# A block with RWKV-7 heads on one core: doublings of the triangular inverse for two chunks at a time, and three generators for a chunk's preparation instead of two

## The chip, the cores and the metric

The kernel runs on one core of a Trainium2 chip. The metric is the device time of one execution in microseconds (us), as the median over runs.

## What is computed

Two layers of a trunk over 1280 tokens of 1024 features: 256 tokens of context, then 1024 latent ones. Each layer normalises, multiplies by one combined input projection, gives its columns to three groups of heads (gated linear attention, windowed softmax attention, RWKV-7 in both directions), multiplies what they return by one output projection, adds it, and ends with a SwiGLU network. The part that the change touches is the RWKV-7 recurrence, for 4 heads of 64 features and for both directions:

```python
def step(S, inp):
    rt, wt, kt, vt, kkt, at = inp
    sa = jnp.einsum('bhvk,bhk->bhv', S, kkt)
    S = (S * wt[:, :, None, :] - sa[..., None] * (kkt * at)[:, :, None, :]
         + vt[..., None] * kt[:, :, None, :])
    return S, jnp.einsum('bhvk,bhk->bhv', S, rt)
```

The kernel computes it in chunks of 64 tokens. Within a chunk the updates depend on one another through a strictly triangular 64 x 64 matrix N of each head and direction, and the kernel forms the inverse of (I - N). Everything is float32.

## The kernel before, in words

**The stage.** `mixers` runs, in each layer, the RWKV heads beside the rest of the input projection. The projection has 22 column tiles; nine of them (RWKV's own) come before, and 13 are left for this stage. A column tile is 24 MATMULs for each of three groups of tokens (256, 512 and 512 of them); in the second layer some columns leave the group of 256 out. The last of the 13 (`HOLD = 1`) begins only when the last step of the scan is through. In the text these are the dense products; their tile is `ps_in`.

**The planner.** `Weave` (L669 ff.) writes down the order in which TensorE (PE) takes all this; PE then follows that order strictly. The work is in generators. Each one traces some instructions and then yields either the nanoseconds until its next part has its operands, or a condition on other stages (`after`, `known`). The planner keeps a clock of its own, `TE.t`, which every matmul advances by a fixed estimate (a float32 one with up to 32 rows: 1.06 ns a column; other float32 ones: 1.67 ns a column, at least 130 or 215 ns; dense ones: columns / 2.4 ns; a transpose 108 ns). It takes the part that is ready first and, of those that are ready, the one with the lowest rank; dense products have rank 9 and are always ready. One rule stands above that: where less than `SHARE` = 1000 ns of dense products began within the last 3400 ns of its clock, a dense one goes next. `LEAD` (22000 and 20000 ns by layer) is the time for which dense products run alone at the start. The order on the other engines is left to the framework's scheduler.

**A chunk.** There are NC = 20 steps. In each, both directions do one chunk, and a tile holds four units u (direction, pair of heads).

- `load` (L1105): two DMAs bring `AK`, 256 KB each, from DRAM tensor `d_ab`; `Dt` is copied.
- `prep_a` (rank 2): loads one chunk ahead; waits for the scan of three steps before ("s", i - 3); `gram` makes `LQ` from `AK` (8 matmuls and a masked multiplication on VectorE); `X` starts as the identity, is filled by a select (`copy_predicated`) from `ld`, four ScalarE copies of blocks of `LQ`; then two calls of `level`.
- `level` (L1091): 16 products of 32 x 32 into `ps_y`, a ScalarE copy to `y`, 16 products into `ps_w`, a select into `X` and a transpose into `XT` on VectorE. Each doubles the size of the inverted diagonal blocks. A float32 matmul is two records in the trace, so one such group is "x32".
- `prep_b` (rank 1): after "a" of this chunk and the scan of two steps before; loads v (`VU`, `Vbd`, six DMAs); makes `Ke` on GpSimd; a `level`; the second `gram` (`MP`); a `level`; copies to `XF`; the last doubling (`ps_y6`, `ps_w6`, 8 products each); transposes of `Ke` to `KT`.
- `scan` (rank 0): after "b" of this chunk and the step before: `ps_r` (MP times v, AK times the state `SBD`), copies to `Rbd`, U from `X` (L1218), `VU` copied, `ps_s` from `KT`, the new `SBD` (L1227), and the output rows (L1230 ff.).
- `finish_all` (rank 3): norms of finished token tiles.

`X` and `XT` have two buffers each, `LQ` and `VU` three, `AK` and `y` four. All small PSUM tiles of these generators share a ring of three banks.

```python
def level(lv, LQ, X, XT):
    py = new([P, 4, 32], "ps_y")
    ...
    S.copy(y, py)
    yield 1000
    ...
    V.transpose(f2(XT), f2(X))
    yield 1200
```

Of the kernel before, what the change touches and what calls it, by code (L numbers as in the profile page):

```python
# [57 lines left out]
# column tiles of the input projection, in the order in which they are computed  # L58
# [5 lines left out]
# columns of the per-layer parameter tile  # L64
# [81 lines left out]
def block_kernel(ctx: ExitStack, tc: tile.TileContext, a):  # L146
# [3 lines left out]
    class Tensor:  # L150
        """the tensor engine with an estimate of its time, in ns"""
# [48 lines left out]
    # decay over a chunk, by direction and pair of heads  # L200
# [74 lines left out]
    class Norm:  # L275
        """RMS norm over the features, which lie on the partitions and along k of x"""
# [5 lines left out]
        def add(self, o, g0, n):  # L282
            # apart: not of the ring, whose slots go by the order of the program
# [38 lines left out]
        def modulated(self, l, w_, g0, n, h):  # L322
            """h[:, k, 0 / 1, :] = leading and trailing part of modulate(rmsnorm(x))"""
# [31 lines left out]
    def product(ps, n, wh, k0=0, total=None):  # L355
        """ps[:, :n] = sum over pairs of a weight tile (hi, lo) and activations (hi, lo) in float32 accuracy"""
# [7 lines left out]
    def rsqrt(pool, v, name):  # L364
        """1 / sqrt(v) in place of v, a small tile: bit guess and Newton steps"""
# [26 lines left out]
    # (column of a padded tile, token, tokens)  # L392
    PIECES = [(1, 0, 256), (258, 256, 512), (770, 768, 512)]

    def in_rwkv(l, h, wpool, pool, bpool, cpool, pp, beside, first):
        """the columns of RWKV and what is elementwise in it; the results go to DRAM"""
# [17 lines left out]
        # in the last layer the tokens of the context give keys and values only  # L414
# [3 lines left out]
        def conv(*names):  # L418
            """projection and centred shift of columns; tokens at 1:257 and 258:1282"""
# [29 lines left out]
        def scan_inputs(j, o, t0, n, d):  # L449
            """a, r, kappa and beta of a pair of heads and a direction"""  # L450
# [17 lines left out]
            # exp of the decays up to a token, with a one before the first (forward) or after the last (backward)  # L468
# [73 lines left out]
    def tokens_of(aux, tmp, y, t0, n, dst):  # L542
        """the n columns of y, token-major"""
# [7 lines left out]
    def in_rest(l, h, cols, wpool, pool, own, ypool, pp, spawn):  # L551
        """the other columns, step by step"""
# [6 lines left out]
        def drain(nm, g0, n, ps):  # L559
            # not of the ring for the first columns, whose slots go by the order of the program  # L560
# [61 lines left out]
    def in_gla(l, t0, pool, own, pp, dw):  # L622
        """what is elementwise in the linear attention, for 256 tokens"""
# [38 lines left out]
    def known(at, keys):  # L662
        """for a generator in a Weave: waits for all of the keys (stage, number from 0 on)"""
# [5 lines left out]
    class Weave:  # L669
        """Traces generators in the order in which the tensor engine takes their parts. A generator yields the  # L670
        time until its next part has its operands, or a function that returns the time from which on it has
        them (None: not known yet). Of what is ready, the first in the list goes first."""
# [9 lines left out]
        def run(self, manual=True, stay=()):  # L682
            """until all jobs have ended but those of the ranks that may stay"""
            with tc.manual_schedule(engines={mybir.EngineType.PE}) if manual else nullcontext():
                while any(j[0] not in stay for j in self.jobs):
# [11 lines left out]
                    if self.share:  # L697
                        # the dense matmuls are spread so that the engine's clock stays up
# [15 lines left out]
    def column(mh, t):  # L714
        """the columns of a token tile in the tile of its group"""
# [3 lines left out]
    def mixers(ctx_, l, t_first, ins, h, wpool, dpool):  # L719
        """RWKV beside the rest of the input projection"""  # L720
# [25 lines left out]
    def gla_states(d, t, kt, vt, St, gD, ps_of, into, n=2):  # L746
        """the states (head and key, value) behind the first n chunks of a tile, St the one before them"""
# [12 lines left out]
    def gla_backward(pool, keep_, ps_of, spawn):  # L760
        """the states behind every chunk from the right; returns those after the second and the first of a tile"""
# [26 lines left out]
    def gla_mixer(l, t_first, mh, back, pool, late, pp, spawn):  # L788
# [20 lines left out]
        def forward():  # L809
# [5 lines left out]
            for t in range(NT):  # L815
# [82 lines left out]
        # leading and trailing parts of the values side by side  # L898
# [30 lines left out]
    def swa_mixer(l, t_first, mh, loaded, pools, pp, spawn):  # L929
        # in the order in which what is in them ends  # L930
# [9 lines left out]
        def soft():  # L940
            yield 1000
            for i, (b, kv, j) in enumerate(items):
# [9 lines left out]
                # (place, tokens, key, starts a bank)  # L952
# [16 lines left out]
                if kv == j == 0:  # L969
                    # maximum (negative), sum, sink and 1 / sum of the heads  # L970
# [39 lines left out]
        def values():  # L1010
            o_ = None
            for i, (b, kv, j) in enumerate(items):
# [39 lines left out]
    def rwkv_mixer(l, t_first, pool, fpool, pp, spawn):  # L1052
        """units u = (direction, head pair); heads of a pair lie on the two halves of the partitions"""
# [5 lines left out]
        lev = pool.tile([P, 5, 128], U8, name="lev")  # L1059
        for i in range(5):  # L1060
            lf = pool.tile([P, 2, 64], F32, name="lf")
            o = CO["lev"][0] + i * 256
            SY.dma_start(lf, a["cst"][:, o:o + 256].rearrange("p (d n) -> p d n", d=2)[:, :, 0:64])
            V.tensor_copy(lev[:, i, :], lf.rearrange("p d n -> p (d n)"))
# [6 lines left out]
        XF = [pool.tile([P, 4, 64], F32, name=f"XF{i}") for i in range(2)]  # L1071
# [4 lines left out]
        # times from which on the results of the stages of the steps are there  # L1076
# [12 lines left out]
        blocks = [(u, slice(r, r + 32), slice(r % 64, r % 64 + 32)) for u in range(4) for r in (0, 32, 64, 96)]  # L1089
# [528 lines left out]
```

## Time and profile before

| | |
|---|---|
| median of 3 runs | 3871.54 us (3871.51 to 3885.14) |
| span of the profiled execution | 3864.4 us |
| PE busy | 3708.4 us, 96% |
| VectorE (DVE), ScalarE (ACT), GpSimd (POOL) busy | 49%, 38%, 21% |
| stage of the change, layer 0 / layer 1 | about 319 to 765 us / 2327 to 2770 us |

The profile is of one execution, and its time is given as its span, from the first instruction to the last; the runs have a median 7.1 us above it. "PEld" is the loading of weights, which overlaps the products; "granted clock" is the share of TensorE's full speed that it was given in a stretch, 1.00 being full and 0.50 the lower level. A row of a timeline merges neighbouring instructions of one form. A duration of a merged row runs to the end of its last matmul, which overlaps the start of the next row, so the pace is read from one start to the next.

### The profile page before, as it was taken

To read this page: it belongs to the slowest core of one execution; us is meant where nothing else is said; L and a number is where in the kernel's file an instruction comes from. 1 tells how busy PE (TensorE), PEld (TensorE's weight loads), DVE (VectorE), ACT (ScalarE), POOL (GpSimd) and SP (SyncE) were. 2 spreads that over 40 slices of the span, in tenths; PEclk is the share of its full clock that TensorE was granted. 3 is DMA by queue.
4 is the path that set the end of the run, shared out by engine and by line. 5 is a ranking of instruction groups with operands and counts; after the bars stand their busy time and mean duration, and the time that the engine had idled before them with its cause. 6 is when DMAs were issued, how large, how long until landed. Compare 5 with 4: busy or idle time off the path is not lost. (4 is left out here: it accounts for less than half of the span.)

```text
span 3864.4 us, 75751 instructions
## 1 busy us (share of the span) xinstructions
PE 3708.4 (96%) x31194; PEld 2894.2 (75%) x31194; DVE 1888.0 (49%) x3773; ACT 1457.8 (38%) x3054; POOL 821.6 (21%) x1169
## 2 busy tenths in 40 slices
PE   7999899999999999999999998899999999999998
PEld 4547677767788888888887766677777778888887
DVE  4663545566554333333334783455575643433334
ACT  4333543357334323333333443543375231111113
POOL 3111222211323223323332131222112310000002
PEclk9999999989999999999999999999899999999999
DMA  5454443331311122222211244343322211111111
GB/s 206 148 176 128 119 127 106 85 107 34 117 62 55 61 68 69 69 63 67 70 61 60 80 156 122 107 133 98 89 78 85 83 33 50 40 53 44 55 44 60
DMA packets 264826, 334.96 MB, mean 87 GB/s; under 512 B 48417, under 2 KB 197025, under 8 KB 262433
## 3 DMA queue, kind: packets, MB, share of 16 engines
q1 hardware_dynamic: 264480, 330.12, 27.2%
q8 instruction: 246, 4.03, 0.4%
q14 instruction: 100, 0.81, 0.1%
HBM read 255.15 MB, written 69.64 MB: 84 GB/s over the span
## 5 line engine op out<-in xcount | busy, mean ns | idle before, releaser
L160 PE MATMUL ps_gu<-f,w_hl 128*128 128x512 f32 (+1 forms) x5280 | 1115.9, 371 | 3.8 <-ACT sg L1386 1.5
L160 PEld LDWEIGHTS ps_gu<-f,w_hl 128*128 128x128 f32 x5280 | 914.8, 188 | 184.3 <-ACT w_hl L343 5.9
L160 PE MATMUL ps_in<-h,w_hl 128*128 128x512 f32 (+1 forms) x2928 | 726.2, 385 | 3.4 <-ACT h L331 2.8
L160 PEld LDWEIGHTS ps_in<-h,w_hl 128*128 128x128 f32 x2928 | 485.6, 193 | 161.7 <-issue 86.3
L160 PE MATMUL ps_d<-gt,w_hl 128*128 128x512 f32 (+1 forms) x2688 | 577.9, 371 | 11.0 <-DVE x L1404 9.7
L160 PEld LDWEIGHTS ps_d<-gt,w_hl 128*128 128x128 f32 x2688 | 471.0, 190 | 113.5 <-DVE x L1404 14.0
L1404 DVE SCALAR_TENSOR_TENSOR x<-ps_d,mods,x 128x512 f32<-128x512 f32 (+1 forms) x448 | 306.9, 688 | 344.1 <-PE ps_d L160 343.8
L343 ACT CAST w_hl<-w_raw 128x1024 fp32r<-128x1024 f32 (+2 forms) x214 | 197.4, 942 | 534.8 <-PE ps_d L160 359.6
L242 POOL TENSOR_TENSOR acc_ada<-acc_ada,p_ada 128x256 f32<-128x256 f32 x336 | 262.3, 816 | 612.5 <-ACT p_ada L241 465.1
L344 DVE TENSOR_TENSOR w_hl<-w_raw,w_hl 128x1024 fp32r<-128x1024 f32 (+2 forms) x214 | 238.5, 1122 | 203.2 <-ACT w_hl L343 201.5
L1387 DVE TENSOR_TENSOR sg<-sg,ps_gu 128x512 f32<-128x512 f32 (+1 forms) x110 | 69.8, 635 | 460.5 <-PE ps_gu L160 449.7
L296 POOL TENSOR_TENSOR nacc<-nacc,nsq 128x512 f32<-128x512 f32 (+1 forms) x52 | 60.7, 1167 | 827.1 <-ACT nsq L295 825.0
L1386 ACT ACTIVATE sg<-ps_gu 128x512 f32<-128x512 f32 (+1 forms) x110 | 61.1, 555 | 323.4 <-PE ps_gu L160 321.5
L1388 ACT CAST gt<-sg 128x512 fp32r<-128x512 f32 (+1 forms) x110 | 63.1, 574 | 314.1 <-DVE sg L1387 314.1
L241 ACT ACTIVATE p_ada<-w_ada,cs 128x256 f32<-128x256 f32 x336 | 154.9, 503 | 32.9 <-POOL acc_ada L242 22.7
L160 PE MATMUL ps_o<-m,w_hl 128*128 128x512 f32 (+1 forms) x720 | 164.9, 378 | 0.0
L974 DVE TENSOR_REDUCE mx<-ps_ss 128x1 f32<-128x640 f32 (+2 forms) x144 | 107.6, 747 | 106.9 <-PE ps_ss L160 106.7
L160 PEld LDWEIGHTS ps_o<-m,w_hl 128*128 128x128 f32 x720 | 124.2, 189 | 32.1 <-issue 7.3
L164 PE MATMUL ps_st<-cst,pr 128*128 128x128 f32 x640 | 110.3, 299 | 11.6 <-ACT pr L976 10.3
L976 ACT ACTIVATE pr<-ps_ss,mx 128x640 f32<-128x640 f32 (+2 forms) x144 | 106.0, 737 | 28.1 <-DVE mx L975 25.4
L344 DVE TENSOR_TENSOR pT<-ps_st,pT 128x512 fp32r<-128x512 f32 (+1 forms) x168 | 108.8, 657 | 14.6 <-ACT pT L343 13.7
L343 ACT CAST pT<-ps_st 128x512 fp32r<-128x512 f32 (+1 forms) x168 | 94.4, 565 | 57.0 <-PE ps_st L164 50.1
(289 smaller groups left out, 4793.9 us busy)
## 6 DMA issues: line engine op xcount, KB each, us to landing
w_ada<-in_ada_w_dram SPq DMA_DIRECT2D x192, 256.0 KB, 2.8
w_raw<-in_w_in_dram SPq DMA_DIRECT2D x44, 512.0 KB, 3.8
w_raw<-in_w_gate_dram SPq DMA_DIRECT2D x44, 512.0 KB, 3.6
w_raw<-in_w_down_dram SPq DMA_DIRECT2D x44, 512.0 KB, 3.7
w_raw<-in_w_up_dram SPq DMA_DIRECT2D x44, 512.0 KB, 3.6
AK<-d_ab SPq DMA_DIRECT2D x80, 256.0 KB, 3.2
d_ab<-W SPq DMA_DIRECT2D x16, 1024.0 KB, 4.1
rope<-in_rope_dram SPq DMA_DIRECT2D x20, 512.0 KB, 4.1
```

The source lines that it names most:

```text
L160: return nc.tensor.matmul(out, lhsT, rhs, **kw)
L164: return nc.tensor.transpose(*args)
L241: S.mul(p, w[:, k % 2], cs[:, k, s:s + 1])
L242: G.tensor_tensor(acc[:, s], acc[:, s], p, ALU.add)
L343: S.copy(dst[:, 0], src)
L344: V.tensor_tensor(dst[:, 1], src, dst[:, 0].bitcast(F32), ALU.subtract)
L974: V.tensor_reduce(m_, psf[:, :nk * P], AX.X, ALU.max)
L976: S.activation(pr[:, :nk, :].rearrange("p a n -> p (a n)"), psf[:, :nk * P], AF.Exp, bias=m_, accum_out=mx[:, 1, head:head + 1])
L1386: S.activation(sg[:, :n], pg[:, :n], AF.Silu)
L1387: V.tensor_tensor(sg[:, :n], sg[:, :n], pu[:, :n], ALU.mult)
L1388: S.copy(gt[:, 0, g0:g0 + n], sg[:, :n])
L1404: V.scalar_tensor_tensor(x[:, o, g0:g0 + n], ps[:, :n], mods[:, l, s, 40 + o:41 + o], x[:, o, g0:g0 + n], ALU.mult, ALU.add)
```

## The change

Doublings are made for the chunks 2m and 2m + 1 together. `level` handles tiles with an extra index c for the chunk: 32 products in a group in place of 16, one ScalarE copy, one select and one transpose of 256 columns in place of two of 128 each. `prep_a` goes over 10 pairs: it waits for the scan and for "x" of the pair before (the end of its last doubling), issues the four `AK` loads, yields 3000 ns, then does both grams and two levels. `prep_b` does two levels and the last doubling of the pair and sets "x" for both chunks. What else `prep_b` did (v, `Ke`, `MP`, `KT`) is in a new generator `prep_c`, for one chunk at a time, after "a" of the pair and the scan of two steps before. The scan waits for "x" and "c". Ranks are: scan 0, prep_c 1, prep_b 2, prep_a 2.5, finish_all 3. `X` and `XT` have one buffer each, `LQ`, `VU` and `y` two. `SHARE`, `LEAD` and `HOLD` stay.

```diff
         def level(lv, LQ, X, XT):
-            py = new([P, 4, 32], "ps_y")
-            for u, rs, cs in blocks:
-                TE.matmul(py[rs, u, :], LQ[rs, u, cs], XT[rs, u, :])
-            y = pool.tile([P, 4, 32], F32, name="y", bufs=4)
+            py = new([P, 2, 4, 32], "ps_y")
+            for c, u, rs, cs in blocks:
+                TE.matmul(py[rs, c, u, :], LQ[rs, c, u, cs], XT[rs, c, u, :])
+            y = pool.tile([P, 2, 4, 32], F32, name="y", bufs=2)
             S.copy(y, py)
-            yield 1000
+            yield 1200
...
-            V.copy_predicated(f2(X), lev[:, lv - 1, :], f2(pz))
-            V.transpose(f2(XT), f2(X))
-            yield 1200
+            V.copy_predicated(f3(X), lv_(lv), f3(pz))
+            V.transpose(f3(XT), f3(X))
+            yield 1500
...
         def prep_a():
-            load(0)
-            for i in range(NC):
-                yield after(("s", i - 3))
-                b = batch[i]
-                if i + 1 < NC:
-                    load(i + 1)
+            for m in range(NC // 2):
+                yield after(("s", 2 * m - 3), ("x", 2 * m - 1))
+                load(2 * m)
+                load(2 * m + 1)
+                two = [batch[2 * m + c] for c in range(2)]
+                yield 3000
+                X = pool.tile([P, 2, 4, 32], F32, name="X")
+                XT = pool.tile([P, 2, 4, 32], F32, name="XT")
...
+                LQ = pool.tile([P, 2, 4, P], F32, name="LQ", bufs=2)
+                for c, b in enumerate(two):
+                    gram(b["AK"], 3, LQ[:, c])
...
-                yield 3400
+                yield 3800
                 for lv in range(2, 4):
                     yield from level(lv, LQ, X, XT)
-                b.update(LQ=LQ, X=X, XT=XT)
-                at["a", i] = TE.t + 900
+                for b in two:
+                    b.update(LQ=LQ, X=X, XT=XT)
+                at["a", m] = TE.t + 900
         def prep_b():
+            for m in range(NC // 2):
+                yield after(("a", m), ("s", 2 * m - 3))
+                LQ, X, XT = (batch[2 * m][n] for n in ("LQ", "X", "XT"))
+                for lv in range(4, 6):
+                    yield from level(lv, LQ, X, XT)
+                xf = XF[m % 2]
...
+                S.copy(y, py)
+                yield 1000
+                pz = new([P, 2, 2, 32], "ps_w6")
...
+                for c in range(2):
+                    batch[2 * m + c].update(X=xf[:, c], LQ=LQ[:, c])
+                    at["x", 2 * m + c] = TE.t + 1000
+        def prep_c():
             for i in range(NC):
-                yield after(("a", i), ("s", i - 2))
+                yield after(("a", i // 2), ("s", i - 2))
...
-                VU = pool.tile([P, 512], F32, name="VU", bufs=3)
+                VU = pool.tile([P, 512], F32, name="VU", bufs=2)
...
                 MP = pool.tile([P, 4, P], F32, name="MP", bufs=2)
                 gram(AK, 2, MP)
...
+                yield 1000
                 pt = new([P, 4, P], "ps_kt")
...
+                at["c", i] = TE.t + 1000
...
         def scan():
             for i in range(NC):
-                yield after(("b", i), ("s", i - 1))
+                yield after(("x", i), ("c", i), ("s", i - 1))
...
-        for rank, gen in enumerate((scan(), prep_b(), prep_a(), finish_all())):
+        for rank, gen in ((0, scan()), (1, prep_c()), (2, prep_b()), (2.5, prep_a()), (3, finish_all())):
             spawn(gen, rank, LEAD[l])
```

The masks `lev` are stored twice side by side, and `XF` holds two chunks, so its clearing at the start is twice as wide.

## Rows read from the trace of the kernel before

**Rows 1.** Head of the page.
```profile
span 3864.4 us, 75751 instructions
```
**Rows 2.** Windows over the RWKV stages: us, busy per engine (instructions), PEclk, DMA share, GB/s.
```profile
319.00:756.00 437.00, 407.94 (x8032) 318.97 (x8032) 222.42 (x664) 197.42 (x515) 108.86 (x189) 0.96 0.35 105
2337.00:2771.00 434.00, 400.92 (x7903) 308.87 (x7895) 212.03 (x612) 192.47 (x501) 106.67 (x187) 0.96 0.36 104
```
**Rows 3.** Timeline of PE, layer 0: start, us, line, op, tiles, idle before.
```profile
597.70 1.05 PE L160 MATMUL ps_r<-Vbd,MP 128*128 128x128 f32 x8
...
606.84 0.45 PE L160 MATMUL ps_w<-X,y 32*32 32x32 f32 x32
607.11 0.48 PE L160 MATMUL ps_y<-XT,LQ 32*32 32x32 f32 x32
607.52 1.33 PE L160 MATMUL ps_in<-h,w_hl 128*128 128x256 f32 x9
...
617.13 1.05 PE L160 MATMUL ps_r<-Vbd,MP 128*128 128x128 f32 x8
...
733.52 0.75 PE L160 MATMUL ps_y<-XT,LQ 32*32 32x32 f32 x64
734.20 0.96 PE L160 MATMUL ps_in<-h,w_hl 128*128 128x512 f32 x3
```
**Rows 4.** Windows of PE with tile ps_in alone: us, busy (instructions), PEclk, DMA, GB/s.
```profile
595.80:615.30 19.50, 8.90 (x41) 1.00 0.46 144
756.50:783.00 26.50, 21.78 (x103) 1.00 0.86 204
2364.00:2748.30 384.30, 159.18 (x536) 0.96 0.36 106
2748.30:2770.30 22.00, 0.22 (x1) 0.84 0.39 101
```
**Rows 5.** Groups by line and form, whole run: busy, mean ns | idle before, releasers.
```profile
L160 PE MATMUL ps_y<-XT,LQ 32*32 32x32 f32 x5760 | 87.1, 196 | 17.3 <-DVE XT L1102 15.8 <-DVE rw_rs_y L369 1.5
L160 PE MATMUL ps_w<-X,y 32*32 32x32 f32 x5760 | 84.8, 196 | 9.3 <-ACT y L1175 4.8 <-ACT y L1096 3.1 <-issue 1.1
```
**Rows 6.** Timeline of PE, end of the stage in layer 1.
```profile
2748.36 1.05 PE L160 MATMUL ps_r<-Vbd,MP 128*128 128x128 f32 x8
...
2760.31 1.91 PE L160 MATMUL ps_r<-Vbd,MP 128*128 128x128 f32 x8
...
2770.34 1.89 PE L160 MATMUL ps_in<-h,w_hl 128*128 128x512 f32 x7
```
**Rows 7.** Windows of 2 us within that end, all engines.
```profile
2754.00:2756.00 2.00, 2.00 (x22) 1.69 (x22) 1.94 (x6) 0.50 (x2) 1.74 (x3) 1.00 0.00 0
2760.00:2762.00 2.00, 2.00 (x10) 2.00 (x11) 0.42 (x2) 1.52 (x5) 0.30 (x1) 0.50 0.00 0
```
**Rows 8.** Groups by line and form, whole run, ACT and DVE of a doubling.
```profile
L1096 ACT COPY y<-ps_y 128x128 f32<-128x128 f32 x160 | 42.4, 265 | 142.4 <-PE ps_y L160 140.4
L1175 ACT COPY y<-ps_y 128x64 f32<-128x64 f32 x40 | 8.4, 210 | 15.8 <-PE ps_y L160 15.8
L1101 DVE COPY_PREDICATED X<-lev,ps_w 128x128 f32<-128x128 uint8 x160 | 47.2, 296 | 83.5 <-PE ps_w L160 82.5 <-issue 0.2
L1102 DVE STREAM_TRANSPOSE XT<-X 128x128 f32<-128x128 f32 x160 | 49.2, 308 | 4.1
```
**Rows 9.** Timelines of PE and of SP around loads of AK.
```profile
599.57 1.09 PE L160 MATMUL ps_g<-AK 64*64 64x128 f32 x16
600.36 1.06 SPq L1110 DMA_DIRECT2D AK<-d_ab  x2
...
2327.51 1.97 PE L160 MATMUL ps_g<-AK 64*64 64x128 f32 x16 [5.41 <-DMA AK<-d_ab]
```
**Rows 10.** Page, DMA issues: KB each, median us to landing.
```profile
AK<-d_ab SPq DMA_DIRECT2D x80, 256.0 KB, 3.2
```

More of the change, by code (lines that the diff above doesn't have):

```diff
@@ L1070, in rwkv_mixer @@
         Vbd = [pool.tile([P, 4, P], F32, name=f"Vbd{i}") for i in range(2)]
-        XF = [pool.tile([P, 4, 64], F32, name=f"XF{i}") for i in range(2)]
+        XF = [pool.tile([P, 2, 4, 64], F32, name=f"XF{i}") for i in range(2)]
         for t_ in (R, U, *Vbd, *XF):
@@ L1087, in gram @@
                             mgr.unsqueeze(2).to_broadcast([P, 2, 2, P]), ALU.mult)
[L1089 removed]
+        blocks = [(c, u, slice(r, r + 32), slice(r % 64, r % 64 + 32))
+                  for c in range(2) for u in range(4) for r in (0, 32, 64, 96)]
+        f3 = lambda ap: ap.rearrange("p c u n -> p (c u n)")
+        lv_ = lambda lv: lev[:, lv - 1].rearrange("p c n -> p (c n)")
         def level(lv, LQ, X, XT):
[L1092 to L1095 removed]
+            py = new([P, 2, 4, 32], "ps_y")
+            for c, u, rs, cs in blocks:
+                TE.matmul(py[rs, c, u, :], LQ[rs, c, u, cs], XT[rs, c, u, :])
+            y = pool.tile([P, 2, 4, 32], F32, name="y", bufs=2)
             S.copy(y, py)
[L1097 to L1103 removed]
+            yield 1200
+            pz = new([P, 2, 4, 32], "ps_w")
+            for c, u, rs, cs in blocks:
+                TE.matmul(pz[rs, c, u, :], y[rs, c, u, :], X[rs, c, u, :])
+            V.copy_predicated(f3(X), lv_(lv), f3(pz))
+            V.transpose(f3(XT), f3(X))
+            yield 1500
         def load(i):
@@ L1131, in prep_a @@
                 for r in range(0, 128, 32):
-                    S.copy(ld[r:r + 32], LQ[r:r + 32, :, r % 64:r % 64 + 32])
-                V.copy_predicated(f2(X), lev[:, 0, :], f2(ld))
-                V.transpose(f2(XT), f2(X))
-                yield 3400
+                    S.copy(ld[r:r + 32], LQ[r:r + 32, :, :, r % 64:r % 64 + 32])
+                V.copy_predicated(f3(X), lv_(1), f3(ld))
+                V.transpose(f3(XT), f3(X))
+                yield 3800
                 for lv in range(2, 4):
@@ L1137, in prep_a @@
                     yield from level(lv, LQ, X, XT)
-                b.update(LQ=LQ, X=X, XT=XT)
-                at["a", i] = TE.t + 900
+                for b in two:
+                    b.update(LQ=LQ, X=X, XT=XT)
+                at["a", m] = TE.t + 900
         def prep_b():
+            for m in range(NC // 2):
[4 more added lines that the diff above has]
+                xf = XF[m % 2]
+                for r in (0, 32, 64, 96):
+                    (S.copy if r < 64 else G.tensor_copy)(xf[r:r + 32, :, :, r % 64:r % 64 + 32], X[r:r + 32])
+                ab = [(h, c, v, d) for c in range(2) for v in range(2) for d in range(2) for h in (0, 64)]
+                py = new([P, 2, 2, 32], "ps_y6")
+                for h, c, v, d in ab:
+                    ra, rb = (h, h + 32) if d == 0 else (h + 32, h)
+                    TE.matmul(py[rb:rb + 32, c, v, :], LQ[ra:ra + 32, c, 2 * d + v, rb % 64:rb % 64 + 32],
+                              XT[ra:ra + 32, c, 2 * d + v, :])
+                y = pool.tile([P, 2, 2, 32], F32, name="y6")
+                S.copy(y, py)
+                yield 1000
+                pz = new([P, 2, 2, 32], "ps_w6")
+                for h, c, v, d in ab:
+                    ra, rb = (h, h + 32) if d == 0 else (h + 32, h)
+                    TE.matmul(pz[ra:ra + 32, c, v, :], y[rb:rb + 32, c, v, :], X[rb:rb + 32, c, 2 * d + v, :])
+                for h in (0, 64):
+                    for d in range(2):
+                        ra, rb = (h, h + 32) if d == 0 else (h + 32, h)
+                        (V.tensor_copy if d == 0 else S.copy)(
+                            xf[ra:ra + 32, :, 2 * d:2 * d + 2, rb % 64:rb % 64 + 32], pz[ra:ra + 32])
+                for c in range(2):
+                    batch[2 * m + c].update(X=xf[:, c], LQ=LQ[:, c])
+                    at["x", 2 * m + c] = TE.t + 1000
@@ L1142, in prep_b @@
+        def prep_c():
             for i in range(NC):
[L1143 removed]
+                yield after(("a", i // 2), ("s", i - 2))
                 b = batch[i]
[L1145 to L1146 removed]
+                cc, Dt, AK = (b[n] for n in ("cc", "Dt", "AK"))
+                VU = pool.tile([P, 512], F32, name="VU", bufs=2)
                 vb = Vbd[i % 2]
@@ L1158, in prep_b @@
                                 Dt.unsqueeze(2).to_broadcast([P, 4, P]), ALU.mult)
-                yield from level(4, LQ, X, XT)
                 MP = pool.tile([P, 4, P], F32, name="MP", bufs=2)
                 gram(AK, 2, MP)
-                yield 0
-                yield from level(5, LQ, X, XT)
-                xf = XF[i % 2]
-                for r in (0, 32, 64, 96):
-                    (S.copy if r < 64 else G.tensor_copy)(xf[r:r + 32, :, r % 64:r % 64 + 32], X[r:r + 32])
-                ab = [(h, v, d) for v in range(2) for d in range(2) for h in (0, 64)]
-                py = new([P, 2, 32], "ps_y6")
-                for h, v, d in ab:
-                    ra, rb = (h, h + 32) if d == 0 else (h + 32, h)
-                    TE.matmul(py[rb:rb + 32, v, :], LQ[ra:ra + 32, 2 * d + v, rb % 64:rb % 64 + 32],
-                              XT[ra:ra + 32, 2 * d + v, :])
-                y = pool.tile([P, 2, 32], F32, name="y6")
-                S.copy(y, py)
+                yield 1000
                 pt = new([P, 4, P], "ps_kt")
@@ L1180, in prep_b @@
                 S.copy(KT, pt)
-                yield 300
-                pz = new([P, 2, 32], "ps_w6")
-                for h, v, d in ab:
-                    ra, rb = (h, h + 32) if d == 0 else (h + 32, h)
-                    TE.matmul(pz[ra:ra + 32, v, :], y[rb:rb + 32, v, :], X[rb:rb + 32, 2 * d + v, :])
-                for h in (0, 64):
-                    for d in range(2):
-                        ra, rb = (h, h + 32) if d == 0 else (h + 32, h)
-                        (V.tensor_copy if d == 0 else S.copy)(
-                            xf[ra:ra + 32, 2 * d:2 * d + 2, rb % 64:rb % 64 + 32], pz[ra:ra + 32])
-                b.update(VU=VU, vb=vb, KT=KT, MP=MP, X=xf)
-                at["b", i] = TE.t + 900
+                b.update(VU=VU, vb=vb, KT=KT, MP=MP)
+                at["c", i] = TE.t + 1000
         ow = fpool.tile([P, NT, 256], F32, name="ow")
```

19 lines of the change are left out of this document (5 added, 14 removed).

## The prediction
> **What bounds the kernel now.** I read the page first: the span is 3864.4 us [rows 1]. Next the table of windows, to find where TensorE (PE) is not at full speed. The diff touches only the RWKV stage of each layer, and there PE is busy 407.9 of 437 and 400.9 of 434 us at a granted clock of 0.96 [rows 2]: 29.1 + 33.1 = 62.2 us idle, and 2 x 0.04 x 871 = 70 us in the lower of its two levels (1.2 GHz; 1.00 is 2.4). Eight MATMULs of ps_r take 1.05 us at 1.00 [rows 3] and 1.91 us at 0.50 [rows 6, 7], so those 70 us lose 70 x (1 - 1.05/1.91) = 31 us. About 93 us in both layers is thus all that smoother work could win; the rest is PE work, which the change keeps.
>
> Then the timeline of PE. A step of the scan takes 617.13 - 597.70 = 19.4 us at full clock [rows 3], with dense products of the input projection in every hole: 8.9 us of 19.5 [rows 4]. So RWKV itself needs 10.6 us a step, 21 us for two chunks. By the table by tile, dense products are a stock that ends: layer 0 still has 103 - 72 = 31 of them when the last step begins (72 are the held column), layer 1 has one in the last 22 us [rows 4].
>
> What happens without them is the end of layer 1: from 2748.36 to 2770.34 [rows 6], 22.0 us hold ten groups of eight 128-column MATMULs (10 us at full clock), a gram (1.0) and small groups and transposes (3.3), 14.3 us at full speed; the ratio is 1.54. The clock goes to 0.50 there [rows 7].
>
> **The order.** PE's order is written by the planner, so its constants decide who runs out. Check on the old code: a step costs it 13.0 us (scan 4.29, two grams 3.42, eight level products 4.34, last doubling and transposes 0.97), and the rule of 1000 ns dense in 3400 makes that 13.0 / 0.706 = 18.5, with some 5.7 us dense (whole MATMULs). A dense column is 12.8 us to it (48 x 213 ns + 24 x 107). Layer 1 has 138 us; 20 go in the lead, about 13 before the first step: 105 / 5.7 = 18.5 steps. The trace runs out at the nineteenth [rows 4, 6].
>
> The new code by the same constants: the doublings of a pair must end ("x") before those of the next begin, since X has one buffer. The chain for a pair is load 3.0 + grams 3.4 + 3.8 + four levels of 1.09 + 1.2 + 1.09 + 1.5 + handover 0.9 + last doubling 0.54 + 1.0 + 0.54 + 1.0 = 33.7 us. Higher ranks and due dense parts delay it: a scan product before the load 1.7, a dense part or scan product before three level products 2.7, prep_c's grams, transposes and a dense part before both products of the next level 3.7: 8.2 with roundings. So the planner's pair period is 41.9 us instead of 36.9; 26.05 are RWKV, 15.8 dense instead of 11. Until the first "x" 22 (20) + 20.1 us of dense go. Layer 0: 153.6 - 42.1 = 111.5, or 7.05 of the nine periods between pairs; layer 1: 98.1, or 6.2. So 1.95 + 2.8 = 4.75 pair periods and the last two steps of each layer run without dense products.
>
> **The change part by part.**
> - Periods without dense products: 21 x 1.54 = 32.3 us on the chip against 21 of work: 11.3 each, 54 for 4.75. Ends: 6 each (only idle from the copies between products) and 21 (the last step of before, 2760.31 to 2770.34, takes 10.0 us for 5 of work [rows 6]). I take 1.54, being the nearest mixture of work.
> - Last two steps: 5 us too long each by that same step, 20 for both layers, less 22.0 - 14.3 = 7.7 that layer 1 pays already: +12 (2 to 20).
> - Levels for two chunks. The ACT copy takes 265 ns for 128 columns and 210 for 64 [rows 8], so some 370 for 256; the DVE select and transpose (296 and 308) at most double. Instructions halve, ACT and DVE get lighter; costed at nothing in itself, as both are busy half the stage at most [rows 2]. What counts is PE's waits: small products waited 17.3 and 9.3 us, 26.6 of the 62.2 idle [rows 5]; that share of the clock's 31 us is 13. Half as many waits in other work that stays: -20 (0 to -40). Where one goes, the next late thing is R's copy or the gated attention's products, left as they are.
> - Against that stands a row: waits are for ACT and DVE that are half idle [rows 2, 5], and merged instructions are longer, 0.1 + 0.6 us a level. The Trainium skill (Perfetto Trace Analysis, Optimizing Scalar/DVE Operations) says that where these engines are not saturated yet hold others up, breaking instructions up may help; this change merges them. By that rule 80 pair levels would lose up to 80 x 0.7 = 56 us instead of winning 20; no trace here shows it, as dense products stand between.
> - Groups of small products: x32 costs 0.27 us when another small group follows (606.84 to 607.11) and 0.41 before a full-size product (607.11 to 607.52); x64 costs 0.68 (733.52 to 734.20) [rows 3]. Two joined save 0 to 0.14; 200 joins: 0 to -28, taken as -8.
> - AK loads. Before, a chunk ahead; now four 256 KB loads, then 3.0 planned us, then the grams. SP issued two at 600.36, 0.8 us behind the gram at 599.57 that follows them in the program [rows 9], 0.53 each, landing in 3.2 [rows 10]: 5.1 us where 3.0 planned are about 3.6 of PE's time. Queued behind a late gram is all of PE. 0 (SP was ahead) to 1.5 us for 20 pairs: 0 to +30, taken as +8. In layer 1 the first gram waits 5.41 us for AK [rows 9]; now some 14 dense products go first: -3.5.
> - The d_v loads, Ke and MP in prep_c: "c" needs only "a", two levels ahead of "x", so six DMAs of a chunk gain time; nothing, within the range. Masks, wider XF and its clearing: hidden under the 20 us lead, else 1 us.
>
> Sum: 54 + 12 + 8 - 20 - 8 - 3.5 = +42.5. The profiled span lies 7.1 us under the median 3871.5 of the runs; the sum is set on the median: **3914 us**.
>
> **The rivals.**
> - Smooth tail (faster). Place: the periods without dense. If the chain alone keeps the clock at 1.00, they cost 6 each, 29 + 2; if all small waits go (-40), joins pay 28 and the start 5: -42, 3829 us. It decides where a pair without dense takes under 27 us. For: the chain by durations, 20 us, is shorter than planned. Against: [rows 6, 7] fell to 0.50.
> - The order is not as I read it: the planner's pair stays at 36.9, and the dense stock lasts. Then -31 + 8: 3848. Against: the check on the old code; the least chain, 33.7, is below 36.9, so it hangs on my 8.2 of delay.
> - Even: tail at 6 each (-25), all small waits gone (-20): 3869.
> - Late AK in place of late copies: +30 instead of +8, 3936.
> - Longer chain through merged instructions (the rule above): +56 for -20, about 3990. Against: planned gaps were widened with them.
>
> **How the numbers follow.** Forecast 0.50 (own range 3880 to 3960), late AK 0.08, longer chain 0.05, smooth tail 0.18, other order 0.11, even 0.08. About 0.5% (19 us) is what a measurement of this kernel tells from no change. Faster by more: smooth tail and half of the other order, 0.23. Within: even, the other half, and 0.06 from the forecast's low end, 0.19. Slower: 0.58. The range must reach into the faster cases and cover the tail's price: 3835 to 3980 leaves out about 2 in 10.
>
> **What would show it.** Right: dense products of the projection end some 80 us before the last ps_s of layer 0 and 105 us before that of layer 1; there pairs of steps take about 32 us with the clock partly at 0.50; in front of that pairs take 39 to 40 us with less idle in ps_y and ps_w than 26.6 us. Grams waiting on AK by 0.4 us on average. Wrong: dense products beside the last pairs; clock 1.00 without them; more idle before ps_y and ps_w than now.

## The result and the profile after

The changed kernel takes **3928.2 us** (median of 4 runs, 3906.3 to 3938.4) against 3871.5 us in the runs beside it: ratio 1.0135, 95% interval [1.0112, 1.0158], 56.6 us slower. The forecast was 3914, slower. The profiled execution is 69.8 us longer than that of before, so it overstates the difference by 13 us. Its page and its groups, beside [rows 1, 5, 8]:

```profile
span 3934.2 us, 75044 instructions
...
PE 3717.8 (94%) x31194; PEld 2931.1 (75%) x31194; DVE 1867.7 (47%) x3533; ACT 1417.2 (36%) x2794; POOL 814.4 (21%) x1109
```
```profile
L160 PE MATMUL ps_g<-AK 64*64 64x128 f32 x1280 | 91.5, 292 | 8.7 <-DMA AK<-d_ab 7.7 <-DVE MP L1086 0.8 <-DVE in L577 0.3
L160 PE MATMUL ps_w<-X,y 32*32 32x32 f32 x5760 | 74.4, 199 | 22.1 <-ACT y L1165 9.7 <-ACT y L1100 8.3 <-issue 4.0
L160 PE MATMUL ps_y<-XT,LQ 32*32 32x32 f32 x5760 | 73.2, 197 | 46.0 <-DVE XT L1106 27.9 <-DVE rw_rs_t L373 7.4 <-DVE XT L1139 6.1
...
L1105 DVE COPY_PREDICATED X<-lev,ps_w 128x256 f32<-128x256 uint8 x80 | 35.6, 445 | 74.2 <-PE ps_w L160 73.0
L1106 DVE STREAM_TRANSPOSE XT<-X 128x256 f32<-128x256 f32 x80 | 35.5, 444 | 2.2
L1100 ACT COPY y<-ps_y 128x256 f32<-128x256 f32 x80 | 29.8, 372 | 114.7 <-PE ps_y L160 114.2
```

The merged instructions did what they were meant to: 372, 445 and 444 ns for 256 columns, far less than twice the 265, 296 and 308 of [rows 8], and the small products themselves are 171.9 - 147.6 = 24.3 us less. But the waits in front of them, which were to halve, went from 17.3 + 9.3 = 26.6 us [rows 5] to 46.0 + 22.1 = 68.1.

**Where in the stage.** I cut the RWKV stage of each layer at the first products (`ps_r` from `Vbd`) of steps 0, 6 and 12 and at the last `ps_s`, and asked the table of windows of both kernels for the three stretches (us, busy time per engine, granted clock, DMA share, GB/s). Before, layer 0 and layer 1:

```profile
344.29:484.86 140.57, 126.87 (x2435) 96.91 (x2427) 72.31 (x209) 81.64 (x191) 36.12 (x67) 0.96 0.36 107
484.86:617.13 132.27, 122.87 (x2408) 97.41 (x2406) 63.84 (x146) 58.14 (x157) 36.60 (x61) 0.94 0.42 131
617.13:762.84 145.71, 140.04 (x2699) 111.19 (x2698) 80.61 (x292) 52.59 (x151) 35.73 (x59) 0.98 0.27 78
...
2359.72:2505.92 146.20, 130.17 (x2439) 97.95 (x2429) 65.14 (x159) 79.89 (x186) 36.70 (x67) 0.95 0.33 99
2505.92:2632.85 126.93, 118.28 (x2367) 91.41 (x2366) 64.44 (x143) 56.25 (x149) 36.81 (x59) 0.95 0.44 134
2632.85:2766.63 133.78, 128.51 (x2627) 101.33 (x2627) 74.38 (x288) 49.95 (x146) 31.32 (x58) 0.99 0.28 80
```
After:
```profile
356.87:541.49 184.62, 156.63 (x2544) 123.32 (x2544) 88.78 (x199) 93.17 (x184) 49.19 (x69) 0.91 0.41 124
541.49:675.53 134.04, 128.81 (x2494) 105.31 (x2493) 50.80 (x91) 45.33 (x104) 26.39 (x43) 1.00 0.34 98
675.53:796.22 120.69, 95.41 (x2279) 81.70 (x2277) 65.18 (x241) 31.66 (x83) 26.94 (x45) 0.84 0.26 71
...
2410.55:2592.49 181.94, 155.09 (x2509) 120.49 (x2508) 79.73 (x149) 90.48 (x174) 49.09 (x67) 0.91 0.43 128
2592.49:2714.12 121.63, 117.65 (x2421) 95.43 (x2420) 45.53 (x83) 41.92 (x97) 23.55 (x40) 0.98 0.32 94
2714.12:2830.61 116.49, 89.11 (x2267) 76.77 (x2261) 64.88 (x238) 30.84 (x82) 27.40 (x46) 0.87 0.22 61
```

What is lost in a row is its length less PE's busy time, and 0.45 of its time at the lower clock (2 x (1 - clock) x length; 0.45 = 1 - 1.05/1.91, as in the prediction). For both layers together, after less before:

| steps | idle | time at 0.50 | loss |
|---|---|---|---|
| 0 to 5 | 29.7 to 54.8 us | 25.9 to 66.0 us | **+43** |
| 6 to 11 | 18.1 to 9.2 us | 28.6 to 4.9 us | **-20** |
| 12 to 19 | 10.9 to 52.7 us | 8.5 to 68.9 us | **+69** |

With 3 us more ahead of step 0 this is 95; from the first gram to the last `ps_s` the two stages became 53.5 us longer (473.1 + 463.3 against 443.8 + 439.1). So PE seems to have had some 42 us less to do in them: 24 are the joined groups. The rest I can't assign. Some 4 us of it come from the formula, which counts idle time at the lower clock in both columns and takes 0.45 where the eight MATMULs of `ps_r` below, at 2.08 us instead of 1.05, give 0.50: with only PE's busy time at the lower clock, at 0.50, the 95 are 91.

**The end of the stage** is what was forecast. By the timeline of PE in layer 0 the last dense products are two at 686.33, 110 us before the last `ps_s`; in layer 1 they are at 2701.89, 129 us before:

```profile
686.33 0.73 PE L160 MATMUL ps_in<-h,w_hl 128*128 128x512 f32 x2
686.90 1.05 PE L160 MATMUL ps_r<-Vbd,MP 128*128 128x128 f32 x8
...
696.42 1.09 PE L160 MATMUL ps_g<-AK 64*64 64x128 f32 x16
700.02 1.28 PE L160 MATMUL ps_y<-XT,LQ 32*32 32x32 f32 x64 [2.52 <-DVE rw_rs_t L373]
...
711.34 2.08 PE L160 MATMUL ps_r<-Vbd,MP 128*128 128x128 f32 x8
...
717.07 1.94 PE L160 MATMUL ps_r<-Rbd,XF 128*64 128x128 f32 x8 [1.51 <-ACT Rbd L1230]
...
747.50 2.08 PE L160 MATMUL ps_r<-Vbd,MP 128*128 128x128 f32 x8
```

The waits of 1.5 to 2.5 us have nothing beside them, and the same eight MATMULs that took 1.05 us at 686.90 take 2.08 at 711.34 and 747.50: the granted clock is at its lower level. A pair takes 747.50 - 711.34 = 36.2 us there.

**The first six steps** were not in the forecast. Waits of PE in layer 0 (total us, times, longest), before in 344.3 to 484.9 and after in 356.9 to 541.5:

```profile
PE ps_gl L160 <- ACT vt L548: 5.5, 4, 2.7
...
PE ps_y L160 <- DVE XT L1102: 1.3, 1, 1.3
```
```profile
PE ps_gl L160 <- ACT vt L548: 11.6, 6, 5.7
PE ps_y L160 <- DVE XT L1106: 9.1, 4, 2.9
```

`ps_gl` belongs to the gated attention (`in_gla`, L622 ff.), which runs beside the first columns. In layer 1 the same two waits go from 5.9 and 0.8 us to 13.4 and 6.0. How the gated attention makes a doubling late can be read from one wait of 2.24 us, on three engines:

```profile
397.83 0.75 PE L160 MATMUL ps_w<-X,y 32*32 32x32 f32 x64
398.51 2.11 PE L160 MATMUL ps_in<-h,w_hl 128*128 128x512 f32 x8
402.86 0.74 PE L160 MATMUL ps_y<-XT,LQ 32*32 32x32 f32 x64 [2.24 <-DVE XT L1106]
...
399.51 0.69 DVE L642 TENSOR_TENSOR_SCAN gl_u<-cst,gl_z 128x256 f32<-128x256 f32 x1
401.53 0.17 DVE L650 COPY dD<-gl_e 128x4 f32<-128x4 f32 x1 [1.33 <-ACT gl_e L645]
401.61 0.43 DVE L1105 COPY_PREDICATED X<-lev,ps_w 128x256 f32<-128x256 uint8 x1
402.27 0.44 DVE L1106 STREAM_TRANSPOSE XT<-X 128x256 f32<-128x256 f32 x1
...
399.79 1.28 ACT L645 ACT_TABLE_LOAD   x1
```

`ps_w` was through at 398.6, but the select into X stands on DVE behind the small copy of L650. That one waits 1.33 us for ACT's exponential, which waits for a table load of 1.28 us. Ahead of that copy stands the scan of L642, also of this head. The select starts at 401.61, 3 us late, and PE's eight dense products cover 2.1 of them. Of the seven waits of `ps_y` for this transpose in the first six steps of both layers, six read like this one: ahead of the select stands L650, after 1.0 to 1.8 us of waiting for ACT.

### The profile page after: what moved, and what is told of

Same layout as the page of the kernel before. It is cut to its first block, busy times and chain, and to the rows that moved or that the text cites. A ratio compares the mean times of both kernels' runs of the same rounds, so it can differ in the third digit from the quotient of the medians.

```text
span 3934.2 us, 75044 instructions
## 1 busy us (share of the span) xinstructions
PE 3717.8 (94%) x31194; PEld 2931.1 (75%) x31194; DVE 1867.7 (47%) x3533; ACT 1417.2 (36%) x2794; POOL 814.4 (21%) x1109
## 5 line engine op out<-in xcount | busy, mean ns | idle before, releaser
L160 PEld LDWEIGHTS ps_gu<-f,w_hl 128*128 128x128 f32 x5280 | 915.1, 189 | 184.6 <-ACT w_hl L343 5.9
L160 PE MATMUL ps_in<-h,w_hl 128*128 128x512 f32 (+1 forms) x2928 | 696.9, 382 | 3.4 <-ACT h L331 2.8
L160 PE MATMUL ps_d<-gt,w_hl 128*128 128x512 f32 (+1 forms) x2688 | 576.3, 370 | 11.4 <-DVE x L1420 10.1
L160 PEld LDWEIGHTS ps_d<-gt,w_hl 128*128 128x128 f32 x2688 | 469.5, 189 | 113.9 <-DVE x L1420 14.4
L1403 DVE TENSOR_TENSOR sg<-sg,ps_gu 128x512 f32<-128x512 f32 (+1 forms) x110 | 69.8, 635 | 460.4 <-PE ps_gu L160 448.1
L344 DVE TENSOR_TENSOR pT<-ps_st,pT 128x512 fp32r<-128x512 f32 (+1 forms) x168 | 108.9, 656 | 17.7 <-ACT pT L343 17.2
```

Of the source, the lines that this page charges most:

```text
L160: return nc.tensor.matmul(out, lhsT, rhs, **kw)
L1403: V.tensor_tensor(sg[:, :n], sg[:, :n], pu[:, :n], ALU.mult)
```

## The experiments

The times beside each were those of the kernel before on the same chip, 3869 to 3875 us. For six kernels this is how many dense products (counted as 512 columns) stand in PE's program ahead of the first products of steps 1, 2, 3 and so on:

```
before      L0 28 28 32 27 25 22 31 29 29 29 29 29 29 28 25 25 30 23 28
            L1 28 28 32 27 25 24 28 24 27 29 29 29 27 28 26 31 27 24  0
after       L0 19 68 20 67 16 68 18 64 18 59 17 65 18  0  0  0  0  0  0
            L1 19 70 20 70 15 69 18 61 15 62 18 18  0  0  0  0  0  0  0
two_x       L0 10 46 10 53 11 38 14 50 18 34 12 46 18 32 11 44 10 46 15
            L1 12 36 14 49 10 44 10 45 10 46 10 45 10 46 14 46 11  0  0
gate_only   L0 19 68 20 67 16 68 18 64 18 59 17 65 18  0  0  0  0  0  0
            L1 19 70 20 70 15 69 18 61 15 62 18 18  0  0  0  0  0  0  0
share200    L0 14 47 13 47 13 51 12 51 14 52 14 51 14 47 13 48 13  5  0
            L1 14 47 13 49 14 51 13 52 14 52 14 51 12 50 11  0  0  0  0
after_gl    L0 19 65 16 66 20 67 19 62 17 63 18 66 18  1  0  0  0  0  0
            L1 19 65 16 70 18 67 17 61 16 70 18 18  0  0  0  0  0  0  0
```

**1. Two buffers for X and XT** (SBUF for them comes from `tmp`, with one buffer less, and from `ld`, which shares the ring of `y`).
```diff
-                yield after(("s", 2 * m - 3), ("x", 2 * m - 1))
+                yield after(("s", 2 * m - 3))
-                X = pool.tile([P, 2, 4, 32], F32, name="X")
-                XT = pool.tile([P, 2, 4, 32], F32, name="XT")
+                X = pool.tile([P, 2, 4, 32], F32, name="X", bufs=2)
+                XT = pool.tile([P, 2, 4, 32], F32, name="XT", bufs=2)
```


> The changed kernel, but X and XT have two buffers and the preparation of a pair no longer waits for the last doubling of the pair before (room for it: tmp has one buffer, ld shares the ring of y). In the order that the planner writes, dense products now last to the last step of layer 0 and to step 17 of layer 1, where the changed kernel's end after steps 13 and 12. Theory A (the time goes where the dense products have run out: pairs of steps at 32 to 38 us with the clock partly at 0.50): nearly all of the loss is gone, 3855 to 3875 us. Theory B (the chain of merged instructions is slow by itself, with longer waits before ps_y and ps_w): 3905 us or more, as the merged instructions stay.

Measured: 3867.1 us, 0.9986 [0.9967, 1.0005]. The whole 61 us between the changed kernel and this one hang on two tiles of 1 KB a partition each and on the wait that they make necessary (the gate, in what follows). Its groups:

```profile
L160 PE MATMUL ps_y<-XT,LQ 32*32 32x32 f32 x5760 | 73.2, 197 | 15.0 <-DVE XT L1106 9.6 <-issue 3.5 <-DVE XT L1139 0.9
L160 PE MATMUL ps_w<-X,y 32*32 32x32 f32 x5760 | 73.1, 199 | 24.0 <-issue 11.0 <-ACT y L1100 8.9 <-ACT y L1165 3.7
```

So the change with two buffers is neutral against the kernel before: small products 25.6 us less, but idle time in the two stages 81.7 us against 62.2 from first gram to end, 19.5 more. What joining is worth by itself this doesn't show, since the split and the wider gaps come with it (runs 7 and 8).

**2. The wait without the need for it.** Two buffers as in 1, but the wait for ("x", 2 * m - 1) kept.


> The changed kernel with two buffers each for X and XT, as in two_x, but with the wait for ('x', 2m-1) ahead of prep_a kept, so that the planner still lets one pair begin only when the pair before has left X. TensorE's order is that of the changed kernel step by step (the last dense product stands before step 13 of layer 0 and step 12 of layer 1). Theory A (the time is made by the planned order, which drains the dense products early; the buffer itself delays nothing): 3928 us, 3915 to 3940, dense products gone about 100 us before the last state update of each layer. Rival (TensorE is held up by the single buffers themselves, in waits on the chip): 3867 us as two_x, 3855 to 3885, although the order is the same.

Measured: 3915.7 us, 1.0118 [1.0097, 1.0139]. The planned order alone, with no buffer to wait for on the chip, costs 48.6 of the 61 us. The other 12.5 are not clear of noise: the interval overlaps that of the changed kernel (1.0112 to 1.0158). The first six steps of layer 0 and layer 1 show that the loss there comes with the order too, not with the buffers:

```profile
354.33:536.36 182.03, 151.44 (x2543) 118.39 (x2543) 88.88 (x199) 92.97 (x184) 48.49 (x69) 0.94 0.41 125
...
2391.44:2577.52 186.08, 155.99 (x2508) 121.14 (x2507) 79.83 (x149) 90.42 (x174) 48.65 (x67) 0.90 0.41 125
```

**3. The kernel before with an early start of the dense products.**
```diff
-LEAD = (22000, 20000)
+LEAD = (60000, 58000)
```


> The kernel before with one pair of constants changed: dense products run alone for 60 and 58 us at the start instead of 22 and 20, so that nothing is merged but dense products run out, after step 14 in layer 0 and 11 in layer 1. Theory A: five steps in layer 0 and some five and a half more than now in layer 1 run without them, at about 5.7 us too much each (16.3 us by the ratio 1.54 against 10.6): about 60 us slower than before, 3915 to 3945 us. Theory B: as before, 3872 us, within 10, since the same work is only put in another order.

Measured: 3935.2 us, 1.0171 [1.0147, 1.0194]. A kernel with short doublings and its two buffers, robbed of its last dense products, loses as much as the change does. But the loss is not at the end alone. By the formula of the table its stages have +32 us in steps 0 to 5, -26 in 6 to 11 and +42 in 12 to 19 against the kernel before, the pattern of the change. Steps 0 to 5 of both layers:

```profile
398.16:553.32 155.16, 133.25 (x2441) 101.11 (x2440) 77.22 (x213) 78.52 (x188) 43.89 (x70) 0.89 0.39 118
...
2446.44:2599.12 152.68, 129.01 (x2383) 97.78 (x2382) 72.52 (x164) 73.26 (x177) 40.88 (x68) 0.91 0.41 123
```

So a loss in the first steps needs neither pairs nor the gate. This kernel and the changed one have both taken more dense products by step 6 than the kernel before; whether and how that makes the loss is not shown.

**4. The changed kernel without a head start.**
```diff
-LEAD = (22000, 20000)
+LEAD = (2000, 2000)
```


> The changed kernel with the dense head start cut from 22 and 20 us to 2 in both layers, so that more dense products are left: by the planner's order they end after step 16 in layer 0 and 14 in layer 1 instead of 13 and 12. Theory A: five steps fewer without them at 5.7 us each, 3900 us, within 10; the first gram may wait longer for its operands, which is against it. Theory B: 3928 us, within 10.

Measured: 3935.6 us, 1.0178 [1.0151, 1.0205]: the forecast of 3900 is missed and the time is in the range of theory B, though layer 0's last `ps_s` came at 786.4 instead of 796.2. The head start is itself a cover: inside the two stages this kernel has some 11 us less idle time than the changed one, outside them 20 us more. Ahead of layer 1's RWKV stage PE is left with little, while first DVE and then the DMA engines work (windows of that kernel):

```profile
2320.00:2340.00 20.00, 7.84 (x13) 2.85 (x12) 19.67 (x25) 8.71 (x15) 10.72 (x9) 0.50 0.41 164
2340.00:2360.00 20.00, 13.06 (x50) 7.18 (x51) 4.21 (x7) 3.20 (x6) 7.28 (x21) 0.67 0.74 243
```

So this run doesn't decide about the end of the stage; run 6 does that better.

**5. Shorter planned gaps**, 800 / 900 / 3000 / 1000 ns in place of 1200 / 1500 / 3800 / 3000.
```diff
-            yield 1200
+            yield 800
...
-            yield 1500
+            yield 900
```


> The changed kernel with shorter planned gaps only (levels 800 and 900 ns in place of 1200 and 1500, 3000 in place of 3800 after the grams, 1000 in place of 3000 after the loads): the serial chain of a pair gets shorter in the plan, and dense products last to step 17 of layer 0 and 15 of layer 1 instead of 13 and 12. Buffers, waits and merged instructions are those of the change. Theory A: seven dense-free steps fewer at 5.7 us each, 40 us, less what the too short gaps cost in new waits, up to 20: 3885 to 3910 us. Theory B (merged chain slow by itself; shorter gaps then make it worse): 3928 us or more.

Measured: 3904.4 us, 1.009 [1.0064, 1.0117], as expected. A shorter chain uses less dense work per pair, and it lasts to step 17 and 15; the waits ahead of `ps_y` stay (50.4 us).

**6. The dense products spread thinner, the chain as it is.**
```diff
-SHARE = (1000, 1000)
+SHARE = (200, 200)
```


> The changed kernel with SHARE = (200, 200) in place of (1000, 1000): the chain, its single buffers and its gaps stay, but dense products are no longer put ahead of small work, only into holes. By the planned order a pair of steps now holds about 61 dense products of 512 columns instead of 86, and the stock ends before step 18 of layer 0 and step 15 of layer 1 instead of before steps 13 and 12. Theory A (what costs is that the dense stock is used up too fast, by the dense-heavy first pairs and the bare end): 3885 us, 3870 to 3900, the first six steps of each layer about 150 us instead of 184.6 and 181.9. Rival (the serial chain with its waits for XT costs by itself, wherever the dense products stand): 3915 us or more, the waits ahead of ps_y unchanged near 46 us and the clock at 0.50 as often as before.

Measured: 3908.6 us, 1.0103 [1.0075, 1.0132], between the ranges of theory A and the rival. In layer 0, where the stock now lasts to step 18, the stage takes 448.5 us from first gram to last `ps_s`, against 473.1 in the changed kernel and 443.8 before: nearly the whole cost is gone with the chain and its buffers untouched. In layer 1, which has less and runs out before step 15, it takes 463.7 against 463.3 and 439.1: the first six steps win 26.7 us (155.3), the next six lose 21.9 (143.6), since PE idles there instead (18.5 us). Its waits ahead of `ps_y`:

```profile
L160 PE MATMUL ps_y<-XT,LQ 32*32 32x32 f32 x5760 | 74.3, 198 | 31.1 <-DVE XT L1106 20.3 <-DVE XT L1139 4.6 <-issue 2.7
```

The serial chain wants more dense work than layer 1 has; how it is dealt out only moves the hole.

**7. The split alone:** the kernel before, one chunk at a time, with `prep_b` cut in doublings and the rest (`prep_c`) and the ranks of the change.
```diff
-                yield after(("s", i - 3))
+                yield after(("s", i - 3), ("x", i - 2))
...
+        def prep_c():
...
-        for rank, gen in enumerate((scan(), prep_b(), prep_a(), finish_all())):
+        for rank, gen in ((0, scan()), (1, prep_c()), (2, prep_b()), (2.5, prep_a()), (3, finish_all())):
```


> The kernel before with the generators split as in the change (loads of v, Ke, MP and KT in a prep_c of rank 1, doublings in prep_b of rank 2), but one chunk at a time: no instruction merged. By the planner's order dense products last through layer 0 and to step 17 of layer 1, about as before. Theory A (only running out of dense products costs): 3870 us, within 10. Theory B' (the split puts transposes and grams at bad places, whatever the dense products do): 3890 us or more.

Measured: 3967.1 us, 1.0246 [1.0215, 1.0277], some 97 us over theory A's 3870: the split costs, as theory B' has it, and by far more than its 3890. The largest wait is now for the operand XT (L1134) of the first doubling, which comes later than the 3400 ns planned behind the gram; of the 17.3 us ahead of `ps_y` in [rows 5] none is for it:

```profile
L160 PE MATMUL ps_y<-XT,LQ 32*32 32x32 f32 x5760 | 89.3, 200 | 51.3 <-DVE XT L1134 23.5 <-DVE XT L1102 20.0 <-DVE dD L650 3.2
```

**8. That gap made longer.**
```diff
-                yield 3400
+                yield 4200
```


> split_only with one planned gap longer, 4200 ns in place of 3400 between the first gram and the first level. In split_only PE waits 23.5 us in both layers for the transpose behind that gram (L1134), and the clock falls behind such waits. Theory G (that gap is what the split pushes too close): these waits fall under 8 us, and with them about as much time at the lower clock, some 35 us less, against 17 us more for three more steps without dense products: 3950 us, within 12. Theory S (the split costs at many places, this one not more than others): the waits move elsewhere, and with the longer tail it is 3967 to 3990 us.

Measured: 3919.1 us, 1.0113 [1.0091, 1.0136]; one constant gave 48 us, nearly three times the 17 expected, though the wait went only from 23.5 to 12.2 us:

```profile
L160 PE MATMUL ps_y<-XT,LQ 32*32 32x32 f32 x5760 | 87.0, 200 | 46.6 <-DVE XT L1102 24.5 <-DVE XT L1134 12.2 <-issue 5.3
```

So the gaps of the old code don't fit the new cut (the change itself widens them, to 3800, 1500 and 1200). Where the 48 us came from the traces show only in part: the profiled executions, 3947.8 and 3925.4 us, lie 22 us apart, with the same mean granted clock of 0.961. What the other 49 us of the split are is open.

**9. A smaller share in layer 1 on top of run 1,** `SHARE = (1000, 850)`.


> two_x, with the share of dense products in layer 1 cut from 1000 to 850 ns in 3400, so that they last to the end of layer 1 too (two_x runs its last two steps there without). Theory A: some 8 us less than two_x, 3859 us, within 8, so faster than before by 0.1 to 0.5%. Theory B: as two_x, 3867 us.

Measured: 3872.1 us, 1.0001 [0.9986, 1.0016]: no gain, against theory A.

**10 to 12. A gap in the gated attention,** on the kernel of run 1, on the kernel before and on the changed one.
```diff
             tokens_of(...)
+            yield 3000
```


> two_x with one more planned gap in the elementwise part of the linear attention (in_gla): 3000 ns behind the transposes of one direction, so that PE is not sent to the next direction's product (ps_gl), whose bank is still being read by ACT. PE waits 10.6 and 2.8 us there in two_x, up to 6.8 at once, with the clock at 0.50 behind it. Theory W (what is left to gain is idle PE and the clock behind it): these waits go nearly, 10 to 25 us less: 3845 to 3857 us, faster than before. Rival: the waits only move to the next product that needs ACT, 3867 us, within 7.

> The kernel before with that same gap of 3000 ns in in_gla and nothing else. It waits 7.2 and 9.8 us there. Theory W: 10 to 25 us less than before, 3845 to 3860 us. If both this and two_x_gl gain alike, the gain is not one of the change; if only two_x_gl gains, the pair's fewer waits help. Rival: 3870 us, within 7.

> The changed kernel with one gap more in the gated attention (yield 3000 after the token-major copies of a direction), as in two_x_gl and before_gl. In the changed kernel TensorE waits 25.0 us ahead of ps_gl for ACT's copy vt, 16.7 us more than it should by the waits of two_x_gl (none). Planned order otherwise as in the changed kernel: dense products end before steps 14 and 13. Theory A (in the first six steps of each layer the loss comes from the gated attention's own short waits, which the denser stream of columns brings closer together): the 25 us ahead of ps_gl go and little comes in their place; 3906 us, 3895 to 3916. Rival (the waits pass on to the doublings, whose select stands behind the gated attention's work on DVE): 3918 to 3940, with ps_y and ps_w waiting more than the 68 us of the changed kernel.

Measured: 3874.4 us, 1.0009 [0.9995, 1.0024]; **3861.8 us, 0.9978 [0.9965, 0.999]**; 3939.7 us, 1.0172 [1.0129, 1.0214]. Run 10 gained nothing; run 11 gained 8.5 us, just short of the 10 to 25 of theory W. On the kernel before, it removes the wait (17.0 to 2.6 us ahead of `ps_gl`) and brings the granted clock of the two stages to 0.99 and 0.98, from 0.96 in [rows 2]; this is the fastest kernel of the study. Its stages:

```profile
319.00:765.00 446.00, 424.65 (x8140) 331.45 (x8139) 231.29 (x729) 204.96 (x534) 108.45 (x191) 0.99 0.37 110
2327.00:2770.00 443.00, 413.88 (x8008) 317.62 (x8006) 225.10 (x674) 199.05 (x514) 111.11 (x189) 0.98 0.38 108
```

On the changed kernel the waits ahead of `ps_gl` fall as well, from 25.0 to 7.6 us (the "16.7" in that expectation is a slip; all 25 were meant), and nothing is won: `ps_y` and `ps_w` wait nearly as long as before (44.6 + 17.2 us), and the median is 11.5 us higher, a difference that the two intervals, which overlap, leave open. The time is the rival's, its sign (more than 68 us there) is not. In the trace the first six steps get 17.5 us shorter (178.6 + 170.5 us), but the gated attention reaches further into steps 6 to 11, which get 21.9 us longer (142.3 + 135.3; idle 18.5 us instead of 9.2). So taking away the waits ahead of `ps_gl` alone moves the loss and doesn't end it.

## Why the prediction was right, and where it was not

**The order: right.** The forecast read from the planner's constants that a pair whose doublings must end before the next begin takes longer in the planner's clock, uses more dense work, and leaves the end of each layer bare. It named 80 and 105 us; 110 and 129 came, as a pair takes 86 dense products (68 + 18), 18.4 us, not 15.8. 15 steps are bare instead of 13.5. Runs 1 and 2 show the cause of the slowdown: without the gate it is gone, and with the gate alone most of it is there.

**The price of a pair without dense work: right.** 32.3 us were taken from 22.0 / 14.3 of [rows 6]. Measured: 36.2, 33.1 (layer 0), 31.8, 37.9 and 32.8 (layer 1), mean 34.4. The two terms for the end, 54 + 12 = 66 us, answer to the +69 of the table, for 15 bare steps where 13.5 were forecast.

**The term of -20 for fewer small waits: half right, and the step that failed.** It was for "other work that stays", as if all pairs before the end were alike. In steps 6 to 11 the loss fell by 20 us. In steps 0 to 5 it rose by 43. There the gated attention shares PE, DVE and ACT, PE's waits ahead of `ps_gl` more than doubled (11.4 to 25.0 us in both layers), and the select that a whole pair waits for stands behind it on DVE. The forecast named those products as "next late" and priced them at nothing. Six steps take 184.6 and 181.9 us, 61 a pair, where 39 to 40 were forecast; with the gate gone (run 1) they take 143.7 and 139.9. The row on which the forecast's price of a step rests is step 11 [rows 3, 4], behind the gated attention, which ends in the steps 7 and 8; the kernel before needs 140.6 and 146.2 us for the first six steps, 47 to 49 a pair. That the order makes this loss is shown by runs 1 and 2. That the gated attention is what carries it is read from the waits and not shown by a run: run 12 took most of the waits ahead of `ps_gl` away and the time did not fall, and run 3 has a loss of +32 us there without pairs.

**The joins: too small.** -8 was taken from 0 to -28; the groups show -24.3. With the rest of the work that PE did not have in the stages (some 42 us in all by the table) this nearly cancels the +43. So the sum of 42.5 lies near the 56.6 measured although two of its terms are off, by 43 and by some 34 us: the size was partly luck.

**AK: nothing.** In layer 0 no gram waits over 0.3 us in sum, where +8 was set. The start of layer 1 was to win 3.5 and lost 2.3 on [rows 9]'s 5.41: no dense products go right ahead of the grams; the next ones stand in PE's timeline behind them, at 2371.05.

```profile
2367.28 3.84 PE L160 MATMUL ps_g<-AK 64*64 64x128 f32 x32 [7.67 <-DMA AK<-d_ab]
2371.05 1.16 PE L160 MATMUL ps_in<-h,w_hl 128*128 128x256 f32 x4
```

**The rivals.** The smooth tail is out (clock 0.84 and 0.87 in the last eight steps), as is the other order. The longer chain through merged instructions, for which the Trainium skill (Perfetto Trace Analysis, Optimizing Scalar/DVE Operations) was named, is not borne out: run 1 merges as much and is even (0.9986). Of the three signs that were to speak against the forecast one came, more idle time before `ps_y` and `ps_w`; it is the term of -20 that it speaks against.

## What to carry to other kernels

Where a planner deals out filler work, a buffer count is a planning constant: what one buffer less cost in waits on the chip was not clear of noise (12.5 us), but it made the planned chain longer, and the longer chain drew the filler into the first steps and left none for the end, for 49 us. Count the filler per step in the program's order before and after (a table of one line a kernel), and look for the stretch where a second consumer, here the gated attention, shares the engines on which the chain's operands are made. When a chain is re-cut, its gaps belong to the cut: 800 ns in one place were worth 48 us.

## What was not expected of the hardware

Fewer waits came with much more clock: in run 11 the waits ahead of `ps_gl` are 14.4 us shorter than in the kernel before, and the granted clock of the two stages is 0.99 and 0.98 instead of 0.96, which is 27 us at the lower level instead of 70 [rows 2]. The time of the kernel fell by 8.5 us only. In the first six steps of the changed kernel's layer 0 PE is busy 156.6 of 184.6 us at a granted clock of 0.91; in steps 6 to 11 it is busy 128.8 of 134.0 us at 1.00. And an ACT table load of 1.28 us in one head's work stands in the chain, through DVE, that ends two engines further on in a wait of PE of 2.24 us.
